# An encoder block on one core: output weights summed by transfers in DRAM instead of on VectorE, a fixed order for the opening, and a new table for the scan's order

## The chip, the cores and the metric

The kernel runs on one core of a Trainium2 chip. The metric is the device time of one execution in microseconds (us). Five engines with their own instruction queues matter here: TensorE (PE), VectorE (DVE), ScalarE (ACT), GpSimd (POOL) and SyncE (SP, which only issues transfers). Sixteen DMA engines serve the transfers that SP, ACT and POOL issue.

## The reference

One layer of a hybrid encoder over 1040 tokens (16 learned meta tokens and 1024 frames) of width 1024, in float32:

```
h = concat(meta, x)
u = rmsnorm(h) ; proj = u @ w_in                   # q, k, v, o and gates of 4 + 4 heads
h_ml = mlstm(conv+silu(q,k), v, gates)             # heads 0..3, chunked state scan
h_rt = retention(rotary(q), rotary(k), v)          # heads 4..7, chunked state scan
mixed = concat(sigmoid(o) * norm(h_ml), silu(g) * norm(h_rt))
h = h + mixed @ w_out
h = h + (silu(conv(rmsnorm(h) @ w_up)) * (rmsnorm(h) @ w_gate)) @ w_down
out = rmsnorm(h)[16:]
```

## The kernel before

Each float32 operand of a large product is split into a high part (`hi`, rounded by a cast) and a low part (`lo`, the difference), and each product is three matmuls, hi x hi, hi x lo and lo x hi. The large products use a seven-product (Strassen-like) scheme on 2 x 2 blocks, so that sums of blocks of the weights and of the activations are needed beside the blocks.

The program has four stages. **The opening** (0 to about 57 us) loads x in five regions of tokens (`RNG`, regions 0 to 4), forms the rms norm of each region, scales it, casts it to the high part and subtracts for the low part, while PE forms the value product of head 4 (`pv`) and its q and k product (`pq`, weights `("q4", 0)` and `("q4", 1)`). PE begins with products of a zero tile (`zeros`). **The projection and scan stage** (to about 650 us) runs, for the heads in the order 4, 0, 1, 2, 3, 5, 6, 7, the products q, v and o; between them it deals the scans of the heads done so far: for each chunk of 128 tokens the scores `s`, the weighted scores `pt`, their split `ph` and `pl` (on POOL, L1636 and L1655), the split of the values `vh` and `vl` (on POOL, L1667 and L1668), the products `u` and `n`, and the state `C`. Which scan step stands between which matmuls is decided when the program is written, by a planner (`slot`, `tick`) that keeps an estimated load per engine and follows the table `RULES`: seven numbers for each pair (kind of product, head), among them how long a step may lag and how many steps may be dealt in one slot. Once dealt, each engine runs its instructions in that order. **The output projection** `w_out` follows, then the **feed-forward stage** to the end.

The seven-product scheme for `w_out` needs sums of blocks of its weights. Before, eight units `w_unit(k)`, k = 0 to 7, are dealt into the projection stage: each loads two pieces of `w_out` to SBUF (2 x 512 KB), adds four times 128 x 512 elements on DVE (L651, L652, L654, L655) and stores four sums of 256 KB to DRAM (L658), where the output projection reads them later. The sums for `w_down` are made in another way, by `wsum`, from about 900 us: three copies from DRAM to DRAM and four transfers that add to their destination, all issued by POOL (L674 and L667).

The splits of a weight piece are in `parts`: casts on ACT (L484) and subtractions on DVE (L489). In the opening `norm_sums(2, True)` folds the squares of region 2 on DVE (L890, L893), PE sums them over partitions (L848), ACT and DVE form 1/rms, PE spreads it (L861) and DVE scales x (L920); the low parts of region 2 are L936.

Of the kernel before, what the change touches and what calls it, by code (L numbers as in the profile page):

```python
# [17 lines left out]
P = 128  # L18
# [70 lines left out]
def body(ctx, tc, h_in, vecs, cst, mask_in, rot, w_v0, w_vp, w_g, w_out, w_up, w_gate, w_down, out):  # L89
# [14 lines left out]
    def after(later, first):  # L104
        dep(later, first, False)
# [212 lines left out]
    jslot = {}  # L318
    age = {}
    jfreed = [[0, 1], [2, 3]]  # L320
    jcap = [2]

    def job(nm, *srcs):
        jobs.append((nm, srcs))
        return len(jobs) - 1
# [155 lines left out]

    def parts(key, pairs, src):
        for i, (hi, lo) in enumerate(pairs):
            m = AC.copy(hi, src[:, i * HB:(i + 1) * HB])  # L484
            if not dealt[0]:
                after(m, last["first" if key[0] == "q4" else "raw" if key[2] == 4 else "late"])
        yield
        for i, (hi, lo) in enumerate(pairs):
            m = V.tensor_tensor(lo, src[:, i * HB:(i + 1) * HB], hi.bitcast(F32), ALU.subtract)  # L489
            if not dealt[0]:  # L490
                after(m, last["added"])
        done.add(key)
# [149 lines left out]
    def w_unit(k):
        js = [job(f"w{k + 8 * i}", w_out[k + 8 * i]) for i in range(2)]

        def make():
            def g():
                ask(js, True)
                yield from landed(*js)
                r1, r2 = (jget(j) for j in js)
                (v11, v21), (v12, v22) = ((r[:, :HB], r[:, HB:]) for r in (r1, r2))  # L650
                V.tensor_tensor(v22, v22, v21, ALU.add)  # L651
                V.tensor_tensor(v21, v21, v11, ALU.add)  # L652
                yield
                V.tensor_tensor(v11, v11, v22, ALU.add)  # L654
                V.tensor_tensor(v12, v12, v11, ALU.add)  # L655
                yield from lag(1.5)
                for x, st_, o in ((v22, "65", HB), (v21, "73", HB), (v11, "65", 0), (v12, "73", 0)):
                    nc.sync.dma_start(sums["w", st_, k][:, o:o + HB], x)  # L658
                yield from lag(4)
                jfree(*js)  # L660
            spawn(g())
        unit(("w", k), 0, make)
# [18 lines left out]

# [68 lines left out]
    wk_ = list(range(8))  # L750

    def w_units(n):
        return [lambda: w_unit(wk_.pop(0))] * n

    def m_units(h):
        return [lambda: m_unit(h)]
    u_fm("o", 4, *v_units(0, 0), *w_units(1))
    prev = 4
    for p, (a, b) in enumerate(PAIRS):
        u_fm("q", a)  # L760
        u_vp(p)
        u_fm("o", a, *v_units(p, 1), *m_units(prev), *w_units(1))
        u_fm("q", b, *(r_units(0, 1) if p == 2 else w_units(1)))
        u_fm("o", b, *(v_units(p + 1, 0) if p < 2 else r_units(2, 3)), *m_units(a), *w_units(p < 2))
        prev = b
    u_fm("q", 7, *r_units(4, 5))
    u_fm("v", 7, *r_units(6, 7))
# [105 lines left out]
    def norm_sums(r, late=False):  # L873
# [34 lines left out]
        norm_scale(r)  # L908
        norm_lows(r)

    def norm_scale(r):
        half, j0, j1 = RNG[r]
        if len(norms[r]) < 3:
            norm_rows(r)
        xs, got, pr = norms.pop(r)
        parts_ = [[u[:, :, j0:j1] for u in UB[f"{half + 1}{i + 1}"]] for i in range(2)]
        scaled[r] = xs, parts_
        for i, x in enumerate(xs):
            for k in range(4):
                last["scale"] = V.scalar_tensor_tensor(x[:, k], x[:, k], vec[:, V_MIX + 4 * i + k:V_MIX + 4 * i + k + 1], pr, ALU.mult, ALU.mult)  # L920
# [1047 lines left out]
    need(("q4", 1), 0)
    row.clear()
    quiet = last["added"]  # L1970
    raw_done(1, pv1, col0[:, 1:2])
# [7 lines left out]
    raw_done(2, pv2, col1[:, 0:1])  # L1979
    for i in range(2):  # L1980
        after(AC.copy(w0hi[i], w0raw[i]), last["cast"])
    pair = q4_pair(0, 0, 272, [next(ring0), next(ring0)], 2, third)
    next(pair)
    norm_scale(2)
# [798 lines left out]
```

## Time and profile before

| quantity | value |
|---|---|
| median of 3 runs | 1500.06 us (1500.03 to 1500.83) |
| profiled execution, its own time | 1501.6 us |
| its span in the trace | 1499.8 us |
| PE busy in the span | 1477.2 us (98%) |
| DVE, ACT, POOL busy | 74%, 51%, 13% |

The profile is of one execution; its own time is 1.8 us above its span and 1.5 us above the median of the runs. Busy time of PE counts matmuls that are pipelined, so that a busy PE can still run below its pace, at the lower of its two clocks for example.

### The profile page before, as it was taken

Reading aid. Unit: us, or ns where it says so; the run is one execution under the profiler, and the core shown is the slowest. Engines: PE = TensorE matmul, PEld = TensorE weight load, DVE = VectorE, ACT = ScalarE, POOL = GpSimd, SP = SyncE. Lnnn points to the kernel's source line nnn. Section 1 sums busy time; section 2 is a strip of 40 time slices with the busy share of each in tenths; the row PEclk is TensorE's granted clock in tenths of the full one; section 3 lists DMA queues with packets and bytes.
Section 4 is the critical chain, followed back from the end, with each engine's and each line's share of the span. In section 5 each row is a group of like instructions: output and inputs, shape, how many; then the busy total and the mean of one; then the engine's idle time right before and its main releaser. Section 6 shows DMA issues by size and latency. Waiting matters only on the chain.

```text
span 1499.8 us, 26297 instructions
## 1 busy us (share of the span) xinstructions
PE 1477.2 (98%) x10034; PEld 1342.3 (89%) x10034; DVE 1113.5 (74%) x2142; ACT 759.4 (51%) x1471; POOL 190.3 (13%) x406
## 2 busy tenths in 40 slices
PE   9999999999999999999999999999999999999997
PEld 7989999999899989987888999888888889888887
DVE  6987878788778776857867887666666666777667
ACT  6566555565555455544454664444444445444443
POOL 0003220314031303040000002222210000000000
PEclk9999999999999999999999999999999999999999
DMA  6021364224523354697333258888762225933313
GB/s 236 28 86 66 121 200 153 79 78 168 185 85 114 126 199 147 206 399 259 106 107 130 96 173 215 217 214 203 186 157 77 75 81 186 354 99 106 99 43 113
DMA packets 97758, 223.85 MB, mean 149 GB/s; under 512 B 10600, under 2 KB 25648, under 8 KB 97456
## 3 DMA queue, kind: packets, MB, share of 16 engines
q1 hardware_dynamic: 82992, 191.68, 37.7%
q0 software_dynamic: 8448, 23.07, 7.7%
q10 hardware_dynamic: 6192, 7.41, 1.4%
q8 instruction: 79, 1.29, 0.4%
q14 instruction: 47, 0.39, 0.1%
HBM read 178.05 MB, written 67.15 MB: 163 GB/s over the span
## 4 chain that ended last, share of the span: by engine, by line
PE 88%; DVE 7%; DMA 3%; issue 1%; ACT 1%; SPq 0%; DVEq 0%; POOL 0%; ACTq 0%
PE pdx L954 3%; PE pdx L953 3%; PE pdx L952 3%; PE pup_x L953 3%; PE pup_x L952 3%; PE pup_x L954 3%; PE pga_x L952 2%; PE pga_x L953 2%; PE pga_x L954 2%; PE pdy L954 2%; PE pdy L953 2%; PE pwx L954 2%; PE pdy L952 2%; PE pwx L952 2%; PE pwx L953 2%; PE n L1701 2%
## 5 line engine op out<-in xcount | busy, mean ns | idle before, releaser
L794 ACT CAST hi_up<-raw_up 128x512 fp32r<-128x512 f32 (+1 forms) x52 | 36.5, 720 | 110.2 <-PE pga_z L953 61.1
L795 DVE TENSOR_TENSOR lo_up<-raw_up,hi_up 128x512 fp32r<-128x512 f32 (+1 forms) x52 | 41.3, 808 | 38.4 <-ACT hi_up L794 37.6
L953 PE MATMUL pup_x<-ul_g,hi_up 128*128 128x256 f32 (+1 forms) x240 | 67.4, 282 | 0.0
L952 PE MATMUL pup_x<-uh_g,hi_up 128*128 128x256 f32 (+1 forms) x240 | 67.2, 282 | 0.0
L795 DVE TENSOR_TENSOR lo_ga<-fraw_ga,hi_ga 128x512 fp32r<-128x512 f32 (+1 forms) x51 | 40.6, 799 | 35.5 <-ACT hi_ga L794 35.3
L954 PE MATMUL pup_x<-uh_g,lo_up 128*128 128x256 f32 (+1 forms) x240 | 66.4, 282 | 0.0
L795 DVE TENSOR_TENSOR lo_d<-rd,hi_d 128x1024 fp32r<-128x1024 f32 (+1 forms) x34 | 37.6, 1112 | 32.8 <-ACT hi_d L794 32.7
L954 PE MATMUL pdx<-uh_d,lo_d 128*128 128x512 f32 (+1 forms) x156 | 57.9, 375 | 0.0
L794 ACT CAST hi_ga<-fraw_ga 128x512 fp32r<-128x512 f32 (+1 forms) x51 | 35.4, 713 | 44.4 <-PE pup_z L953 23.9
L953 PE MATMUL pdx<-ul_d,hi_d 128*128 128x512 f32 (+1 forms) x156 | 57.8, 374 | 0.0
L794 ACT CAST hi_d<-rd 128x1024 fp32r<-128x1024 f32 (+1 forms) x34 | 32.3, 960 | 48.2 <-PE pdy L953 32.5
L954 PE MATMUL pdy<-uh_d,lo_d 128*128 128x512 f32 x132 | 51.9, 393 | 0.0
L953 PE MATMUL pdy<-ul_d,hi_d 128*128 128x512 f32 x132 | 51.7, 392 | 0.0
L2650 POOL TENSOR_TENSOR resid<-resid,Rc 128x256 f32<-128x256 f32 x2 | 1.4, 716 | 381.3 <-ACT Rc L865 381.3
L674 POOL DMA_DIRECT2D wsd<-w_down_d x33 | 19.9, 746 | 231.0 <-DVE s2up L2408 230.8
L952 PE MATMUL pdx<-uh_d,hi_d 128*128 128x512 f32 (+1 forms) x156 | 48.5, 372 | 0.0
L1636 POOL CAST ph<-pt 128x128 fp32r<-128x128 f32 x64 | 20.0, 312 | 221.0 <-DVE pt L1644 132.9
L952 PE MATMUL pdy<-uh_d,hi_d 128*128 128x512 f32 x132 | 47.9, 389 | 0.0
L952 PE MATMUL pga_x<-uh_g,hi_ga 128*128 128x512 f32 x120 | 47.5, 396 | 0.0
L953 PE MATMUL pga_x<-ul_g,hi_ga 128*128 128x512 f32 x120 | 47.5, 396 | 0.0
L954 PE MATMUL pga_x<-uh_g,lo_ga 128*128 128x512 f32 x120 | 47.1, 393 | 0.0
L1668 POOL TENSOR_TENSOR vl<-v,vh 128x258 fp32r<-128x258 f32 (+1 forms) x48 | 36.1, 752 | 80.2 <-PE n L1675 54.0
(1737 smaller groups left out, 6020.4 us busy)
## 6 DMA issues: line engine op xcount, KB each, us to landing
raw_up<-w_up_d SPq DMA_DIRECT2D x22, 512.0 KB
fraw_ga<-w_gate_d SPq DMA_DIRECT2D x22, 512.0 KB
acts<-cv SPq DMA_DIRECT2D x44, 256.0 KB
wsd<-w_down_d POOLq DMA_DIRECT2D x44, 256.0 KB, 6.7
rd<-wsd SPq DMA_DIRECT2D x22, 512.0 KB
raw_w<-w_out_d SPq DMA_DIRECT2D x20, 512.0 KB
wsw<-raw_w SPq DMA_DIRECT2D x32, 256.0 KB
raw_m<-w_out_d SPq DMA_DIRECT2D x14, 512.0 KB
```

The source lines that it names most:

```text
L674: dep(G.dma_start(x, y), last["pace"], True)
L794: AC.copy(hi[:, o:o + n], x)
L795: V.tensor_tensor(lo[:, o:o + n], x, hi[:, o:o + n].bitcast(F32), ALU.subtract)
L952: m.append(PE.matmul(pt, ah, xh_, start=first and k == 0, stop=False, skip_group_check=True))
L953: PE.matmul(pt, ah, xl_, start=False, stop=False, skip_group_check=True)
L954: m.append(PE.matmul(pt, al, xh_, start=False, stop=last and k == n - 1, skip_group_check=True))
L1636: G.tensor_copy(ph, pt)
L1668: G.tensor_tensor(low, v, vh.bitcast(F32), ALU.subtract)
L1701: PE.matmul(pn[:L, :nv], qd, state["C"][:, :nv], start=False, stop=True)
L2650: nc.gpsimd.tensor_tensor(RES[mb][:, a0:t1], RES[mb][:, a0:t1], R[1], ALU.mult)
```

## The change

1. The eight `w_unit(k)` are gone from the projection stage. A new `w_sums(range(8))` stands in the opening, behind the low parts of region 2: 24 copies from DRAM to DRAM, issued by SP, each of which waits until DVE has written those low parts (`last["lows", 2]`), and 32 adding transfers, issued by POOL, in three rounds over the eight k.
2. The opening is written in one fixed order up to the squares of region 3: 11 products of zero rather than 13, the norm's sums of region 0 behind one product of the values rather than three, the low part of region 0's first half ahead of region 1's scaling, the fold of region 2 ahead of the splits of the q weights, the gates' scalings (`raw_g`) behind. The two casts of the first q weights go from ACT to POOL. Region 2 of x is loaded ahead of the second q weights.
3. 18 of the rows of `RULES` have other numbers, so that the planner deals the scan anew.

```diff
-    ('q', 0): (3, 0.5, 2.0, 2.0, 3, 1, 3),
+    ('q', 0): (3, 0.3, 4.5, 4.0, 3, 0, 3),
...
-    jcap = [2]
+    jcap = [1]
...
-            m = AC.copy(hi, src[:, i * HB:(i + 1) * HB])
+            m = G.tensor_copy(hi, src[:, i * HB:(i + 1) * HB]) if key == ("q4", 0) else AC.copy(hi, src[:, i * HB:(i + 1) * HB])
...
+    def w_sums(ks):
+        for k in ks:
+            d65, d73 = (sums["w", x, k] for x in ("65", "73"))
+            for x, y in ((d65, w_out[k]), (d73[:, HB:], w_out[k][:, HB:]), (d73[:, :HB], w_out[k + 8][:, :HB])):
+                dep(nc.sync.dma_start(x, y), last["lows", 2], True)
+        for step in range(3):
+            for k in ks:
+                d65, d73 = (sums["w", x, k] for x in ("65", "73"))
+                if step == 0:
+                    add(d65[:, HB:], w_out[k + 8][:, HB:])
+                    add(d73[:, HB:], w_out[k][:, :HB])
+                else:
+                    add((d65, d73)[step - 1][:, :HB], (d65[:, HB:], d65[:, :HB])[step - 1])
...
-    u_fm("o", 4, *v_units(0, 0), *w_units(1))
+    u_fm("o", 4, *v_units(0, 0))
...
     xload(2)
+    jcap[0] = 2
+    jload()
...
-    zeros(13)
+    zeros(11)
     pv1, pv0, pv2 = pp("pv4_1", next(ring0)), pp("pv4_0", next(ring0)), pp("pv4_2", next(ring0))
-    raw_value(pv1, xg0, META, (0, 1, 2))
+    raw_value(pv1, xg0, META, (0,))
...
     norm_lows(2)
-    next(pair, None)
     fourth = norm_sums(3, True)
     last["third"] = last["added"]
+    w_sums(range(8))
```

DVE in the opening, from the reciprocal of region 1's norm on; `u11l` and `u12l` are low parts, `sqr` the squares that are folded, `lo_q` the low parts of the q weights, `gts` the gates. Before:

```order
L852 RECIPROCAL rcola_229<-rcola_229 128x1
L1920 TENSOR_TENSOR x_129<-sig,pra_301 128x4x128
L1920 TENSOR_TENSOR x_128<-sig,pra_301 128x4x128
L1929 TENSOR_TENSOR u11l<-x_129,u11h 128x4x144
L1929 TENSOR_TENSOR u12l<-x_128,u12h 128x4x144
L1915 TENSOR_SCALAR gts<-pv_1_255,rcola_228 128x2x4
L1929 TENSOR_TENSOR u11l<-x_129,u11h 128x4x128
L1929 TENSOR_TENSOR u12l<-x_128,u12h 128x4x128
L489 TENSOR_TENSOR lo_q_0_0_324<-raw_q_0_213,hi_q_0_0_323 128x512 x2
L890 TENSOR_TENSOR sqr_139<-sqr_139,sqr_140 128x4x256
L893 TENSOR_TENSOR sqr_139<-sqr_139 128x2x256
L489 TENSOR_TENSOR lo_q_1_0_336<-raw_q_1_215,hi_q_1_0_335 128x512 x2
```

The same place of DVE in the changed program (whose lines have other numbers):

```order
L845 RECIPROCAL rcola_229<-rcola_229 128x1
L1929 TENSOR_TENSOR u11l<-x_129,u11h 128x4x144
L1920 TENSOR_TENSOR x_129<-sig,pra_304 128x4x128
L1920 TENSOR_TENSOR x_128<-sig,pra_304 128x4x128
L1929 TENSOR_TENSOR u12l<-x_128,u12h 128x4x144
L1929 TENSOR_TENSOR u11l<-x_129,u11h 128x4x128
L1929 TENSOR_TENSOR u12l<-x_128,u12h 128x4x128
L884 TENSOR_TENSOR sqr_139<-sqr_139,sqr_140 128x4x256
L887 TENSOR_TENSOR sqr_139<-sqr_139 128x2x256
L494 TENSOR_TENSOR lo_q_0_0_301<-raw_q_0_213,hi_q_0_0_300 128x512 x2
L845 RECIPROCAL rcola_358<-rcola_358 128x2
L494 TENSOR_TENSOR lo_q_1_0_330<-raw_q_1_219,hi_q_1_0_329 128x512 x2
```

One low part moved ahead of region 1's scaling; the fold (L884, L887) moved ahead of the first `lo_q`, and the gates' scaling is no longer in front of it.

POOL between the opening and the scan of head 4, from the second split of head 4's values on; `v_10` and `v_00` are value tiles of head 0. Before:

```order
L1667 CAST vh_2_1399<-v4lo 128x256
L1608 MEMSET vz 16x2
L1117 MEMSET v_10_1852 128x4x2
L1117 MEMSET v_00_1622 128x4x2
L1636 CAST ph_1_1362<-pt_1_1350 128x128
L1655 TENSOR_TENSOR pl_1_1363<-pt_1_1350,ph_1_1362 128x128
```

In the changed program 32 adding transfers stand between the same cast and `v_10`; these are the first of them:

```order
L1663 CAST vh_2_1425<-v4lo 128x256
L650 DMA wsw_0_159<-w_out_d 128x512
L650 DMA wsw_0_167<-w_out_d 128x512
L650 DMA wsw_1_160<-w_out_d 128x512
L650 DMA wsw_1_168<-w_out_d 128x512
L650 DMA wsw_0_159<-wsw_0_159 128x512
L1604 MEMSET vz 16x2
L650 DMA wsw_2_161<-w_out_d 128x512
L650 DMA wsw_2_169<-w_out_d 128x512
L650 DMA wsw_3_162<-w_out_d 128x512
L650 DMA wsw_1_160<-wsw_1_160 128x512
```

`ph_1`, which the scan's first product with whole chunks needs, now stands behind all 32. On PE that product, `n_1`, stands 24 rows nearer to the start of the program than before (row 476, not 500), most of them matmuls of 264 columns or fewer.

DVE in the o product of head 3, around the first evacuation of `po3y`; `raw_w` are the sums of `w_unit`. Before:

```order
L651 TENSOR_TENSOR raw_w_5258<-raw_w_5258,raw_w_5256 128x512
L652 TENSOR_TENSOR raw_w_5256<-raw_w_5256 128x512
L1047 TENSOR_TENSOR sig<-sig,po3y_5279 128x258
L489 TENSOR_TENSOR lo_o_4_0_5238<-raw_o3b,hi_o_4_0_5237 128x512
L654 TENSOR_TENSOR raw_w_5256<-raw_w_5256,raw_w_5258 128x512
L655 TENSOR_TENSOR raw_w_5258<-raw_w_5258,raw_w_5256 128x512
L1047 TENSOR_TENSOR sig<-sig,po3y_5301 128x256
L1232 SCALAR_TENSOR_TENSOR kT_5273<-rawk,vec,kT_5273 128x527
L1232 SCALAR_TENSOR_TENSOR kT_5273<-rawk,vec,kT_5273 128x526
L1232 SCALAR_TENSOR_TENSOR kT_5273<-rawk,vec,kT_5273 128x525
L489 TENSOR_TENSOR lo_o_4_0_5238<-raw_o3b,hi_o_4_0_5237 128x512
```

And in the changed program:

```order
L1228 SCALAR_TENSOR_TENSOR kT_5215<-rawk,vec,kT_5215 128x527
L1228 SCALAR_TENSOR_TENSOR kT_5215<-rawk,vec,kT_5215 128x526
L1228 SCALAR_TENSOR_TENSOR kT_5215<-rawk,vec,kT_5215 128x525
L1043 TENSOR_TENSOR sig<-sig,po3y_5277 128x258
L494 TENSOR_TENSOR lo_o_2_0_5149<-raw_o3a,hi_o_2_0_5148 128x512
L494 TENSOR_TENSOR lo_o_4_0_5234<-raw_o3b,hi_o_4_0_5233 128x512
L1043 TENSOR_TENSOR sig<-sig,po3y_5293 128x256
L494 TENSOR_TENSOR lo_o_4_0_5234<-raw_o3b,hi_o_4_0_5233 128x512
```

The four additions are gone from between the pieces of `lo_o`, and the convolution (L1232, now L1228) stands ahead of `po3y`. At the same place of head 6's o product the piece `lo_o_2` moved ahead of the evacuation of `po6y`, and a pair of instructions (a low part and a difference of `raw_fr`, 128 x 512 each) from ahead of it to behind it.

## Rows read from the trace of the kernel before

**Rows 1.** The page, busy time: us, share of the span, instructions.

```profile
PE 1477.2 (98%) x10034; PEld 1342.3 (89%) x10034; DVE 1113.5 (74%) x2142; ACT 759.4 (51%) x1471; POOL 190.3 (13%) x406
```

**Rows 2.** Windows by stage: stretch, its length, busy us of each engine, granted clock, DMA share.

```profile
0.00:115.00 115.00, 109.30 (x817) 101.19 (x818) 95.77 (x194) 67.16 (x127) 5.33 (x24) 0.99 0.36 123
...
160.00:750.00 590.00, 582.07 (x4436) 540.44 (x4435) 456.71 (x989) 314.11 (x640) 116.61 (x274) 1.00 0.49 165
750.00:1400.00 650.00, 649.96 (x3883) 576.36 (x3882) 468.54 (x776) 305.27 (x561) 54.14 (x77) 1.00 0.53 156
```

**Rows 3.** Timeline of PE, opening: start, us, instructions, idle time before and its releaser.

```profile
1.32 5.60 PE L1881 MATMUL pz<-zero 128*128 128x512 f32 x13 [1.32 <-POOL gts L290]
22.26 1.05 PE L848 MATMUL pca<-cs,sqr 128*128 128x1 f32 x8 [0.89 <-DVE sqr L893]
35.91 1.47 PE L848 MATMUL pca<-cs,sqr 128*128 128x1 f32 x12 [0.44 <-DVE sqr L893]
```

**Rows 4.** Windows behind two idle times of PE; the clock is the third number from the end.

```profile
23.00:27.00 4.00, 4.00 (x21) 4.00 (x22) 1.75 (x6) 2.26 (x3) 0.67 (x1) 0.57 0.79 289
560.00:570.00 10.00, 9.28 (x59) 8.36 (x58) 5.92 (x16) 2.73 (x8) 2.44 (x6) 0.83 0.31 105
```

**Rows 5.** Timeline of DVE, opening.

```profile
14.63 1.28 DVE L1920 TENSOR_TENSOR x<-sig,pra 128x512 f32<-128x512 f32 x2 [0.70 <-PE pra L861]
15.84 1.30 DVE L1929 TENSOR_TENSOR u11l<-x,u11h 128x576 fp32r<-128x576 f32 x1
17.06 0.75 DVE L1929 TENSOR_TENSOR u12l<-x,u12h 128x576 fp32r<-128x576 f32 x1
17.73 0.21 DVE L1915 TENSOR_SCALAR gts<-pv,rcola 128x8 f32<-128x8 f32 x1
...
19.07 1.28 DVE L489 TENSOR_TENSOR lo_q<-raw_q,hi_q 128x512 fp32r<-128x512 f32 x2
...
21.52 0.69 DVE L893 TENSOR_TENSOR sqr<-sqr 128x512 f32<-128x512 f32 x1
...
32.58 1.22 DVE L936 TENSOR_TENSOR u12l<-x,u12h 128x1024 fp32r<-128x1024 f32 x1
```

**Rows 6.** Timeline of ACT, then of POOL, opening.

```profile
16.48 1.14 ACT L484 CAST hi_q<-raw_q 128x512 fp32r<-128x512 f32 x2
...
15.79 0.73 POOL L1668 TENSOR_TENSOR vl<-v4lo,vh 128x256 fp32r<-128x256 f32 x1
```

**Rows 7.** Timeline of PE, o products of heads 3 and 6.

```profile
399.82 0.39 PE L954 MATMUL po3y<-uS1h,lo_o 128*128 128x258 f32 x1 [1.80 <-DVE lo_o L489]
...
556.46 0.39 PE L954 MATMUL po6x<-uS2h,lo_o 128*128 128x258 f32 x1 [2.07 <-DVE lo_o L489]
562.00 0.39 PE L954 MATMUL po6y<-uS1h,lo_o 128*128 128x258 f32 x1 [0.72 <-DVE lo_o L489]
```

**Rows 8.** The tile raw_w: durations in ns, min, median, max; first and last start.

```profile
L651 DVE TENSOR_TENSOR raw_w<-raw_w,raw_w x8: 679/687/727, 168.4 to 528.1; 128x512 f32<-128x512 f32 x8
```

**Rows 9.** The page, DMA queue of POOL: packets, MB, share of 16 engines' span.

```profile
q0 software_dynamic: 8448, 23.07, 7.7%
```

**Rows 10.** Timeline of POOL: an adding transfer and the next, which waits for it.

```profile
1106.24 0.81 POOL L667 DMA_DIRECT2D wsd<-wsd  x1 [4.80 <-DMA wsd<-w_down_d]
1111.38 0.83 POOL L667 DMA_DIRECT2D wsd<-wsd  x1 [4.34 <-DMA wsd<-wsd]
```

**Rows 11.** Windows from the low parts of region 2 to the scan of head 4.

```profile
31.00:70.00 39.00, 38.40 (x319) 37.84 (x317) 37.39 (x65) 16.46 (x28) 0.09 (x1) 1.00 0.01 2
70.00:107.00 37.00, 34.59 (x290) 32.91 (x291) 33.20 (x79) 25.94 (x51) 0.10 (x1) 1.00 0.31 101
```

**Rows 12.** Timeline of POOL, then of PE: chunk 1 of head 4.

```profile
110.49 0.29 POOL L1636 CAST ph<-pt 128x128 fp32r<-128x128 f32 x1
...
113.05 0.28 PE L1674 MATMUL n<-vh,ph 128*128 128x256 f32 x1
113.17 0.28 PE L1675 MATMUL n<-vl,ph 128*128 128x256 f32 x1
```

More of the change, by code (lines that the diff above doesn't have):

```diff
@@ L384, in body @@
     evacs = []
+    held = []
     dealt = [False]
@@ L396, in spawn @@
                 owner[id(g)] = key
+        elif held:
+            next(g)
+            held[0].append(g)
         else:
@@ L483, in parts @@
         for i, (hi, lo) in enumerate(pairs):
-            m = AC.copy(hi, src[:, i * HB:(i + 1) * HB])
+            m = G.tensor_copy(hi, src[:, i * HB:(i + 1) * HB]) if key == ("q4", 0) else AC.copy(hi, src[:, i * HB:(i + 1) * HB])
             if not dealt[0]:
-                after(m, last["first" if key[0] == "q4" else "raw" if key[2] == 4 else "late"])
+                if not (held or key == ("q4", 0)):
+                    after(m, last["first" if key[0] == "q4" else "raw" if key[2] == 4 else "late"])
         yield
@@ L640, in m_unit @@
         unit(("m", h), 0, make)
[L642 to L662, printed above, removed]
     sums = {(g, st_, k): dram.tile([P, 2 * HB], F32, name=f"ws{g}{st_}_{k}") for g, n in (("w", 8), ("d", KD)) for st_ in ("65", "73") for k in range(n)}
@@ L749, in body @@
     u_load(("q4", 1), q4[:, 3 * HB:], q4[:, :HB])
-    wk_ = list(range(8))
-    def w_units(n):
-        return [lambda: w_unit(wk_.pop(0))] * n
     def m_units(h):
         return [lambda: m_unit(h)]
-    u_fm("o", 4, *v_units(0, 0), *w_units(1))
+    u_fm("o", 4, *v_units(0, 0))
     prev = 4
@@ L761, in body @@
         u_vp(p)
-        u_fm("o", a, *v_units(p, 1), *m_units(prev), *w_units(1))
-        u_fm("q", b, *(r_units(0, 1) if p == 2 else w_units(1)))
-        u_fm("o", b, *(v_units(p + 1, 0) if p < 2 else r_units(2, 3)), *m_units(a), *w_units(p < 2))
+        u_fm("o", a, *v_units(p, 1), *m_units(prev))
+        u_fm("q", b, *(r_units(0, 1) if p == 2 else ()))
+        u_fm("o", b, *(v_units(p + 1, 0) if p < 2 else r_units(2, 3)), *m_units(a))
         prev = b
@@ L885, in norm_sums @@
         else:
-            after(AC.activation(sq[1], xs[1], AF.Square), last["sqrt"])
+            last["squares"] = AC.activation(sq[1], xs[1], AF.Square)
+            after(last["squares"], last["sqrt"])
         if r == 1:
@@ L909, in norm_split, with norm_scale @@
         norm_lows(r)
-    def norm_scale(r):
+    def norm_scale(r, hook=None):
         half, j0, j1 = RNG[r]
@@ L919, in norm_scale @@
             for k in range(4):
+                if i and k == 0 and hook:
+                    hook()
                 last["scale"] = V.scalar_tensor_tensor(x[:, k], x[:, k], vec[:, V_MIX + 4 * i + k:V_MIX + 4 * i + k + 1], pr, ALU.mult, ALU.mult)
@@ L1887, in region @@
         half, j0, j1 = RNG[r]
-        return [xf[f"{half + 1}{i + 1}"][:, :, j0:j1] for i in (0, 1)], [x[:, :, j0:j1] for x in sqs], tmp.tile([P, 5], F32, tag="rcol", name=f"rcola{r}")
+        return [xf[f"{half + 1}{i + 1}"][:, :, j0:j1] for i in (0, 1)], [x[:, :, j0:j1] for x in sqs], (tmp if r else st).tile([P, 5], F32, tag="rcol" if r else "rraw", name=f"rcola{r}", bufs=2 if r else 1)
     row.append({})
@@ L1911, in raw_meta, with raw_v, raw_g @@
             PE.matmul(pv0[32 * j:32 * j + 32, :264], xg0[i][:, j, :32], w0raw[i][:, j * 264:(j + 1) * 264], start=i == 0, stop=i == 1, tile_position=(0, 32 * j))
-    def raw_done(c, pv, col):
+    def raw_v(c, pv, col):
         AC.activation(vtile[4][0][:, (c - 1) * VW:(c - 1) * VW + DV], pv[:, :DV], AF.Copy, scale=col)
+    def raw_g(c, pv, col):
         V.tensor_scalar(gts[:, :, c, :], pv[:, DV:264].rearrange("p (a b) -> p a b", a=2), col, None, ALU.mult)
@@ L1940, in body @@
     AC.activation(q1[1], x1[1], AF.Square)
-    raw_value(pv1, xg0, META, (3,))
-    raw_meta(0, (0, 1))
+    raw_value(pv1, xg0, META, (1,))
     pr0 = rms_rows(got0, None, "upd")
-    raw_meta(0, (2, 3))
+    raw_value(pv1, xg0, META, (2, 3))
+    raw_meta(0, range(4))
     weighted(xg1, x1, range(4))
@@ L1954, in body @@
     weighted(xg1, x1, (6, 7))
+    low_half(0, 0)
     cast_half(0, 1)
+    held[:] = [[]]
+    issue(1)
+    rest = held.pop()
     pr1 = rms_rows(got1, None, "num")
@@ L1960, in body @@
         cast_half(1, i)
-    for r in range(2):
-        for i in range(2):
-            low_half(r, i)
+    for r, i in ((0, 1), (1, 0), (1, 1)):
+        low_half(r, i)
     raw_value(pv2, xg1, 0, range(8))
     last["first"] = last["cast"]
-    need(("q4", 0), 0)
     third = norm_sums(2, True)
[L1968 to L1971, printed above, removed]
+    held[:] = [[]]
+    issue(2)
+    rest += held.pop()
     t0_ = vz[:META, 264:2 * 264]
@@ L1978, in meta_done, with whole, q4_pass @@
         V.tensor_copy(gts[:META, :, 0, :], t0_[:, DV:].rearrange("p (a b) -> p a b", a=2))
-    raw_done(2, pv2, col1[:, 0:1])
-    for i in range(2):
[L1981 to L1984, printed above, removed]
+    def whole(g):
+        for _ in g:
+            pass
+    qt = [next(ring0), next(ring0)]
+    w = [ready["q4", i] for i in range(2)]
+    pq = [pp(f"pq4{i}00", qt[i])[:, :272] for i in range(2)]
+    def q4_pass(p, i, ks):
+        a, b = ((0, 0), (0, 1), (1, 0))[p]
+        for kb in ks:
+            u = UB[f"1{kb // 4 + 1}"][b]
+            PE.matmul(pq[i], w[i][kb // 4][a][:, kb % 4 * P:(kb % 4 + 1) * P], u[:, kb % 4, :272], start=p + kb == 0, stop=p == 2 and kb == KB - 1, skip_group_check=True)
+    raw_v(1, pv1, col0[:, 1:2])
+    AC.copy(w0hi[0], w0raw[0])
+    raw_v(2, pv2, col1[:, 0:1])
+    for i in range(2):
+        q4_pass(0, i, range(8))
+    q4_pass(1, 0, range(0))
+    whole(rest[0])
+    third()
+    whole(rest[1])
+    AC.copy(w0hi[1], w0raw[1])
+    q4_pass(1, 0, range(0, 8))
+    q4_pass(1, 1, range(0))
+    norm_rows(2)
+    norm_scale(2, lambda: (raw_g(1, pv1, col0[:, 1:2]), raw_g(2, pv2, col1[:, 0:1])))
+    q4_pass(1, 1, range(0, 8))
+    for i in range(2):
+        q4_pass(2, i, range(8))
+    row.clear()
+    AC.copy(raws[0][:, :272], pq[0])
+    after(AC.copy(raws[1][:, :272], pq[1]), last["cast"])
     for i in range(2):
@@ L1993, in body @@
         after(V.tensor_copy(ug[:, 4 * i:4 * i + 4], x[:, :, :META]), last["third"])
-    for c in (3, 4):
-        v4_group(c, next(ring0))
-    pair = q4_pair(0, 272, SB, [next(ring0), next(ring0)], 3, fourth)
+    v4_group(3, next(ring0))
+    v4_group(4, next(ring0), fourth)
+    pair = q4_pair(0, 272, SB, [next(ring0), next(ring0)], 3, lambda: None)
     next(pair)
```

30 rows, old and new, of the table RULES are left out of this document.

## The prediction

> **What bounds the kernel now.** I read the page first, then windows by stage, then the timeline of each engine where PE is idle. On the page PE is busy for 1477.2 of 1499.8 us [rows 1]; what any change can give back is thus some 22 us of idle time, and the stretches in which PE is busy at its lower clock. The windows say where the idle time lies: 115 - 109.3 = 5.7 us before 115 us, 590 - 582.07 = 7.9 us from 160 to 750 us, and nothing in the feed-forward stage, 649.96 of 650 us [rows 2]. So only the opening and the projection stage can pay.
>
> In the opening PE spends 5.60 us on 13 zero products (0.43 us each), and waits twice for a fold of squares on DVE, 0.89 us before 22.26 and 0.44 us before 35.91 [rows 3]. Behind the first wait the granted clock falls: from 23 to 27 us it is 0.57 on average, so part of that time is at the lower level, 1.2 rather than 2.4 GHz, and 4 x (1 - 0.57) = 1.7 us of full-clock work are lost [rows 4]. In the projection stage the largest waits are for low parts of o weights from DVE: 1.80 us at 399.82, 2.07 at 556.46, 0.72 at 562.00 [rows 7]; behind the last two a window of 10 us has the clock at 0.83, again 1.7 us lost [rows 4].
>
> **The opening.** What PE waits for at 22.26 is L893, which ends at 21.52 + 0.69 = 22.21 [rows 5]. In the new order of DVE the idle 0.70 us before 14.63 is filled by a low part that stood behind it, the gates' 0.21 us and the two q splits of 1.28 us come after the fold instead of before it [rows 5]: 2.19 us. The squares that the fold reads must come earlier too; ACT loses the 1.14 us of casts to POOL [rows 6] and one evacuation of values to a later place. Two zero products fewer start everything at most 0.86 us earlier, of which I take 0.3 us, since the norm's sums wait for x and its squares as well. The fold is then done 2.5 us earlier. The gates and q splits that were moved must be done before or between the scalings of region 2, where DVE before waited for PE, so I let the whole 2.5 us reach the second fold at 35.91. From there to 70 us DVE is busy for 37.4 of 39 us [rows 11], and a shift of its chain shifts PE. Bounds: only the wait of 0.89 us goes (PE was slowed by its clock there and not only by the order), or both waits, the lost clock and the two zero products all go: 0.89 + 0.44 + 1.7 + 0.86 = 3.9 us. I take 2.5: it is what the chain gives, and lies between.
>
> One thing speaks against it. POOL's subtraction at 15.79 lasts until 16.52 [rows 6], and the DVE subtraction that starts at 15.84 lasts 1.30 us, where the same shape lasts 0.75 at 17.06 [rows 5]: the two delayed one another by 0.55 us. Moved to POOL, the two q casts can do the same to the folds of regions 0 and 1, once or twice, 0.55 to 1.1 us; one such loss is there already, so I leave it inside the bounds. By the Trainium skill (SBUF — State Buffer, Who interferes with whom) a VectorE instruction with two SBUF inputs contends with a GpSimd instruction that reads SBUF, and one of them blocks for the whole of the other; the trace agrees with the 1.30 against 0.75 us. By that rule alone the opening would give 1.4 us rather than 2.5.
>
> **The w units.** 32 additions of about 0.69 us [rows 8] leave DVE, 22 us, and 16 loads and 32 stores leave SP. Most of this was hidden: DVE is busy for 457 of 590 us there [rows 2] and PE waits only where DVE's order puts a needed low part behind other work. At 399.82 the four additions (2.75 us) stand in front of that low part; without them the wait of 1.80 us goes. At 556.46 no `w_unit` is near, but in the new order a pair of 128 x 512 instructions (2 x 0.69 = 1.4 us) and an evacuation come behind `lo_o_2`; 2.07 us shrink to about 0.3, and with it goes the loss of clock, 1.7 us. Together 1.8 + 1.8 + 1.7 = 5.3 us. A new deal makes waits of its own, which no trace shows: nothing at least, and at most as many as now, 7.9 us [rows 2]. I charge 1.5 us, since most of the 7.9 us are in the places named. Net 3.8 us; from 6.3 us (all three waits, 4.6, and the clock, 1.7, and nothing new) to a loss of 2 us.
>
> **The sums in DRAM.** Copies start when the low parts of region 2 are written, 32.58 + 1.22 = 33.8 [rows 5], less 2.5: at 31.3 us. The DMA engines are idle then (share 0.01 from 31 to 70 us [rows 11]), so the copies alone cost nothing. Their price is in who waits behind them. POOL must issue 32 adding transfers in order, most of which wait for an earlier one, before it comes to `ph_1`. The same work for `w_down`, 11 groups of three copies and four additions, is POOL's whole queue before: 7.7% of the span, 115 us of all 16 engines, 10.5 us a group [rows 9]. Eight groups are 84 us, so they end at 115. One addition takes 1111.38 - 1106.24 = 5.1 us from issue to the release of the next [rows 10]; POOL would have issued the last about 4.3 us before the end, at 111. It is needed when? `n_1` stands at 113.05 now [rows 12]; the opening brings it to 110.55, and the 24 rows fewer ahead of it (0.12 us each by the two rows) by another 2.8 to 107.7; `ph_1` takes 0.29, so POOL must be free by 107.4. That is 3.6 us too late, all of it idle time of PE, which runs in order. [...] From above the loads of 70 to 107 us, 0.31 x 37 = 11.5 us of all engines [rows 11], are in the way as well: POOL free at 122.5, 15.1 us late. I take 2 us, near the lower half, since half of the stretch has no other traffic.
>
> **Sum.** -2.5 - 3.8 + 2 = -4.3 us. Against the profiled execution 1501.6 - 4.3 = 1497.3; the median of the runs stands 1.5 us lower, so 1500.06 - 4.3 = 1495.8 us.
>
> **Rivals.** (a) *POOL's queue decides.* The additions run at the rate of the whole queue and share with the loads, POOL comes to `ph_1` at 122.5, and PE idles 15.1 us at `n_1`: 1500.06 - 2.5 - 3.8 + 15.1 = 1508.9. The point from which the kernel is slower than before is POOL free at 107.4 + 6.3 = 113.7 us. For it: 10.5 us a group is a measured price; the loads for head 0 must pass through the same engines. Against it: an idle stretch of 39 us at the start. By the Trainium skill (DMA: Bandwidth & Descriptors, Queues, rings and completion order) each DMA engine takes turns between the queues that have work, packet by packet, so that these loads would be slowed by the additions too; no row here shows the shares.
>
> (b) *The gains don't arrive.* The fold is earlier, but PE waits as long one step further on (for the scaled region 2, which needs the q splits done first), 0.9 us gained; the new deal has waits of the size of the old, 0.5 gained; POOL costs 1: 1500.06 - 0.4 = 1499.7, no change. For it: DVE is full from 31 to 70 us, so work moved within it is not removed. Against it: 22 us of DVE work are really removed.
>
> (c) *More than forecast*: opening 3.9, middle 6.3, POOL nothing: 1489.9.
>
> **How the numbers follow.** The forecast and its neighbours (1492 to 1498) get 0.52, (c) and near it 0.12, (b) 0.13, (a) and what lies between it and no change 0.23. The range for 8 in 10 goes from (c)'s 1489.9, say 1489.5, to 1504, half of (a)'s loss: beyond are some 0.12 above and 0.05 below. The likeliest case's own range is 1492 to 1498. What a measurement of this kernel can tell from no change is about 0.2%, 3.0 us: below 1497.06 is faster, which takes most of the forecast's chance and all of (c), 0.60; same 0.16; slower 0.24.
>
> **What would show it.** Right: the fold of region 2 ends near 19.7 us and no stretch at the lower clock follows; PE's second fold sums stand near 33.4; no wait of 1.8 us at the o product of head 3 and none over 0.5 at head 6's; POOL issues its last adding transfer before about 109 us and `ph_1` follows when the scores are there. Wrong: a wait of PE for POOL at `n_1` of several us, a DVE wait for A or raw_q0b between 70 and 90 us, because loads come late beside the additions; or new waits for low parts from the new table that add up to more than 4 us.

## The result, and the profile after

The changed kernel takes 1504.12 us (median of 8 runs, 1501.83 to 1507.68), the kernel before 1500.05 us (8 runs on the same chip). The ratio is 1.0028, 95% interval 1.0016 to 1.004: slower by about 0.3%, where I had forecast 1495.8 us and faster. The profiled execution took 1503.68 us with a span of 1501.9 us.

The page of the changed kernel: first busy us, share and instructions of each engine (to be held against [rows 1]), then the granted clock and the DMA share in 40 slices of 37.5 us, then the two large DMA queues (packets, MB, share; [rows 9] has q0 before).

```profile
PE 1475.5 (98%) x10032; PEld 1342.3 (89%) x10032; DVE 1092.0 (73%) x2110; ACT 755.8 (50%) x1468; POOL 216.9 (14%) x440
...
PEclk9999999999999999999999999999999999999998
DMA  7993233223312235697333258888762225933213
...
q1 hardware_dynamic: 78640, 183.29, 36.1%
q0 software_dynamic: 13056, 31.46, 11.2%
```

PE has less to do than before, 1475.5 for 1477.2 us, in a longer span: the loss is idle time and clock. The second and third slices of DMA (37 to 113 us) are full; they are the place to look. The windows by stage of the changed kernel, columns as in [rows 2]:

```profile
0.00:115.00 115.00, 104.85 (x776) 96.29 (x776) 92.88 (x185) 64.50 (x121) 30.72 (x49) 0.97 0.94 247
160.00:750.00 590.00, 588.84 (x4532) 549.62 (x4531) 441.46 (x970) 321.75 (x659) 114.85 (x275) 1.00 0.41 139
750.00:1400.00 650.00, 649.96 (x3884) 576.36 (x3883) 468.51 (x777) 305.25 (x561) 54.12 (x77) 1.00 0.54 156
...
75.00:115.00 40.00, 33.77 (x254) 31.35 (x253) 29.08 (x76) 20.25 (x42) 15.64 (x19) 0.96 0.99 201
115.00:160.00 45.00, 38.48 (x294) 37.39 (x295) 26.73 (x64) 22.28 (x44) 15.76 (x37) 0.92 0.30 79
...
5.00:10.00 5.00, 3.96 (x19) 2.87 (x18) 2.83 (x5) 3.37 (x11) 0.00 (x0) 0.85 1.08 367
10.00:15.00 5.00, 5.00 (x26) 3.55 (x27) 2.94 (x6) 2.86 (x10) 1.38 (x2) 0.81 1.05 370
...
85.00:90.00 5.00, 3.43 (x17) 3.43 (x18) 4.74 (x14) 2.94 (x7) 1.49 (x3) 0.70 1.03 221
...
120.00:125.00 5.00, 3.76 (x16) 3.55 (x17) 1.34 (x5) 0.37 (x1) 3.30 (x9) 0.55 1.08 293
```

From 160 to 750 us PE is idle for 1.16 us, before for 7.93 [rows 2]: that part of the change works better than forecast. Before 160 us it is the reverse: 6.2 us idle from 75 to 115, 6.5 from 115 to 160, and behind both holes the clock is down (0.70 and 0.55). The DMA share before 115 us went from 0.36 to 0.94.

The timeline of PE in the changed kernel names the holes (columns as in [rows 3]):

```profile
1.32 4.53 PE L1879 MATMUL pz<-zero 128*128 128x512 f32 x11 [1.32 <-POOL zero L289]
...
34.71 1.47 PE L841 MATMUL pca<-cs,sqr 128*128 128x1 f32 x12 [0.45 <-DVE sqr L887]
...
86.57 0.39 PE L948 MATMUL po4x<-uS3h,hi_o 128*128 128x256 f32 x1 [4.64 <-ACT sig L1041]
...
121.24 0.58 PE L1670 MATMUL n<-vh,ph 128*128 128x256 f32 x1 [6.81 <-POOL ph L1632]
```

**The second hole** is what I had named rival (a): POOL comes to `ph_1` late. Its timeline, to be held against [rows 10, 12]:

```profile
114.01 0.83 POOL L650 DMA_DIRECT2D wsw<-wsw  x1 [0.30 <-issue]
119.97 0.82 POOL L650 DMA_DIRECT2D wsw<-wsw  x1 [5.13 <-issue]
120.50 0.46 POOL L1113 MEMSET v<- 128x8 f32 x2
120.89 0.29 POOL L1632 CAST ph<-pt 128x128 fp32r<-128x128 f32 x1
```

The 32 additions are issued from 37.16 to 119.97 us; POOL is free at 120.5, where the upper bound in my prediction said 122.5.

**The first hole** begins with a load. Timelines of SP (issue of the copies, then of the two halves of A_4), DVE and ACT in the changed kernel:

```profile
32.63 30.92 SPq L667 DMA_DIRECT2D wsw<-w_out_d  x24
68.71 0.34 SPq L1175 DMA_DIRECT2D A<-rot_d  x1
69.88 0.33 SPq L1176 DMA_DIRECT2D A<-rot_d  x1
...
80.35 0.71 DVE L1252 TENSOR_TENSOR qT<-rawq,A 128x528 f32<-128x528 f32 x1 [3.39 <-DMA A<-rot_d]
83.03 0.71 DVE L1253 TENSOR_TENSOR kT<-kT,A 128x528 f32<-128x528 f32 x1 [1.97 <-DMA A<-rot_d]
...
81.15 0.63 ACT L1249 COPY rawq<-rawk 64x528 f32<-64x528 f32 x1 [3.83 <-DVE qT L1252]
...
85.94 0.31 ACT L1287 ACTIVATE gates<-gates 36x128 f32<-36x128 f32 x1 [1.84 <-DVE gates L1286]
86.16 0.36 ACT L1041 ACTIVATE sig<-po4x 128x256 f32<-128x256 f32 x1
```

A_4 is two transfers of 520 KB. The first is issued at 68.71 and lets DVE go on at 80.35 only, while copies and additions have the DMA engines full; DVE waits for it and for the second half, ACT's copy and its activation of the gates wait for DVE, and the activation that would empty `po4x` stands behind both on ACT, so PE waits.

### The profile page after: what moved, and what is told of

It is laid out like the page before. It is cut to its first block, busy times and chain, and to the rows that moved or that the text cites. A ratio compares the mean times of both kernels' runs of the same rounds, so it can differ in the third digit from the quotient of the medians.

```text
span 1501.9 us, 26232 instructions
## 1 busy us (share of the span) xinstructions
PE 1475.5 (98%) x10032; PEld 1342.3 (89%) x10032; DVE 1092.0 (73%) x2110; ACT 755.8 (50%) x1468; POOL 216.9 (14%) x440
## 4 chain that ended last, share of the span: by engine, by line
PE 90%; DVE 6%; DMA 2%; ACT 1%; issue 1%; SPq 0%; DVEq 0%; POOL 0%; POOLq 0%; ACTq 0%
PE pdx L950 3%; PE pdx L949 3%; PE pdx L948 3%; PE pup_x L949 3%; PE pup_x L948 3%; PE pup_x L950 3%; PE pga_x L948 2%; PE pga_x L949 2%; PE pga_x L950 2%; PE pdy L950 2%; PE pdy L949 2%; PE pwx L950 2%; PE pdy L948 2%; PE pwx L948 2%; PE pwx L949 2%; PE n L1697 2%
## 5 line engine op out<-in xcount | busy, mean ns | idle before, releaser
L788 DVE TENSOR_TENSOR lo_up<-raw_up,hi_up 128x512 fp32r<-128x512 f32 (+1 forms) x52 | 41.4, 810 | 38.3 <-ACT hi_up L787 37.5
L949 PEld LDWEIGHTS pup_x<-ul_g,hi_up 128*128 128x128 f32 x240 | 45.4, 189 | 0.9 <-DVE ul_g L2206 0.2
```

The source lines that it names most:

```text
L788: V.tensor_tensor(lo[:, o:o + n], x, hi[:, o:o + n].bitcast(F32), ALU.subtract)
L949: PE.matmul(pt, ah, xl_, start=False, stop=False, skip_group_check=True)
```

## The experiments

Two theories stood at the start. **A**: the sums in DRAM are the loss, by the time that their transfers take of the DMA engines (A_4 late) and by POOL, which is held in its queue until 120.5 us; opening and scan order gain. **B**: the waits come from the new order itself and the sums lie beside it. All medians and ratios are against runs of the kernel before on the same chip (medians 1499.9 to 1500.3).

**1. No sums.** The sums are left out and the output projection reads unsummed rows:

```diff
-    w_sums(range(8))
...
-                nc.sync.dma_start(x[:, :2 * HB], sums[self.nm, st, k])
+                nc.sync.dma_start(x[:, :2 * HB], w_out[k + 8 * (st == "73")] if self.nm == "w" else sums[self.nm, st, k])
```

> The changed kernel without its 24 copies and 32 additions; the products of the output weights read unsummed rows of w_out in their place (that part of the computation is left out), with as many loads of the same size. Opening and scan order are the changed ones. Theory A (the sums in DRAM hold POOL until 120.5 us and keep the DMA engines full, so that A_4 comes late): both waits of TensorE go, 6.81 us at n_1 and 4.64 us at po4x, and with them the low clock behind them (about 3 us): 1488 to 1491 us. Rival B (the waits come from the new order of the opening, the sums only lie beside them): at least one of the waits stays: 1495 to 1504 us.

Measured: 1490.71 us, ratio 0.9935 (0.9923 to 0.9947). Both holes are gone; windows of 75 to 160 us:

```profile
75.00:115.00 40.00, 36.88 (x287) 34.14 (x287) 31.79 (x84) 22.59 (x48) 3.36 (x9) 1.00 0.31 104
115.00:160.00 45.00, 44.72 (x367) 43.90 (x366) 33.47 (x74) 31.43 (x62) 12.34 (x29) 1.00 0.15 49
```

Against the changed kernel PE has 3.1 us more in the first window and 6.2 in the second, at full clock. B is out: the sums cost 1504.12 - 1490.71 = 13.4 us.

**2. Copies alone.** The sums are not computed; the output projection reads what the copies left:

```diff
+    COPIES_ONLY = True
...
+                if COPIES_ONLY:
+                    continue
```

> The changed kernel with the 24 copies but none of the 32 additions (the sums are left out of the computation). Theory A, in the form that the additions alone hold POOL and carry the DMA load past 64 us: no wait for POOL at n_1, A_4 lands within 3 us of its issue, 1488 to 1491 us. Rival C (the copies' backlog delays A_4 and the loads of q0): the 6.8 us at n_1 go, the 4.6 us at po4x stay: about 1494 to 1496 us.

Measured: 1488.62 us, ratio 0.9919 (0.9906 to 0.9932). The copies cost nothing: the DMA share is 0.15 from 60 to 64 us and 0.00 from 64 to 68, so they are through when A_4 is issued at 69.42. Rival C is out. The DMA queue's row of this kernel from 34 to 62 us, and below it the two queues of the changed kernel from 70 to 115 us (packets, MB, share of 16 engines):

```profile
q1 hardware_dynamic: 2554, 8.26, 91.6%
```

```profile
q0 software_dynamic: 2784, 5.06, 70.4%
q1 hardware_dynamic: 1544, 4.27, 28.6%
```

This gives prices. A copy of 256 KB (0.262 MB) takes 0.916 x 28 / 8.26 x 0.262 = 0.81 us of all 16 engines; an addition of the same size 0.704 x 45 / 5.06 x 0.262 = 1.64 us, twice as much. The eight groups are 8.39 MB of copies, 26 us, and 8.39 MB of additions, 52 us.

**3. The opening alone**, with the units, the old table and no sums in DRAM:

```diff
-    ('o', 0): (4, 0.8, 3.0, 3.0, 4, 0, 1),
+    ('o', 0): (4, 0.3, 3.0, 2.5, 2, 0, 3),
...
+    u_fm("o", 4, *v_units(0, 0), *w_units(1))
...
-    w_sums(range(8))
```

> The changed opening alone: the units that make the sums on VectorE, and the scan order of before, are put back, and no sums in DRAM. Theory A: 1497 to 1499 us, since TensorE's rows up to 69 us stood 2.1 us ahead of before's in the changed kernel. My prediction's term for this part was 2.5 us (1497.5). Rival: the opening brings nothing by itself, as the clock of 0.81 to 0.85 between 5 and 15 us takes it back: 1500 us.

Measured: 1498.29 us (12 runs), ratio 0.9984 (0.9975 to 0.9992): 1.8 us by the medians, 2.4 (1.2 to 3.7) by the ratio. The 12 runs lie between 1495.72 and 1501.63 us, and the profiled one is the slowest of them; its clock is low from 5 to 15 us:

```profile
5.00:10.00 5.00, 3.76 (x18) 2.64 (x16) 2.84 (x5) 2.83 (x10) 0.00 (x0) 0.82 1.08 375
10.00:15.00 5.00, 5.00 (x20) 3.07 (x19) 2.74 (x4) 2.28 (x7) 1.91 (x2) 0.50 1.04 368
```

**4. The same work in two late bursts.**

```diff
-    w_sums(range(8))
...
+            plan.append((COPY_AT + 10.0 * i, lambda k=k: copies(k)))
+            plan.append((ADD_AT[0] + 3.5 * i, lambda k=k: adds(k, 0)))
...
+    COPY_AT = 130 - OFF
+    ADD_AT = [x - OFF for x in (220, 382, 398)]
```

> The changed kernel with the same 24 copies and 32 additions, put later: copies by SP from about 130 to 200 us, additions by POOL from about 220 and from about 382 us, where it has no work of a scan. Theory A: the cost was the place, not the work; as without the sums plus 1 us: 1488 to 1492 us, so faster than both kernels. Rival D (the transfers cost wherever they are, since 16.8 MB more delays the weight loads of 130 to 420 us): new waits for DMA there, 1495 us or more.

Measured: 1500.56 us (12 runs), ratio 0.9999 (0.9989 to 1.0009). Theory A in this form fell: 16 additions in a row make loads late at 220 us as they do in the opening. The rows of ACT and PE there, with DMA queue q0 from 225 to 250 us:

```profile
245.37 0.62 ACT L488 CAST hi_q<-raw_q2a 128x512 fp32r<-128x512 f32 x1 [5.47 <-DMA raw_q2a<-w_g_d]
247.37 0.49 PE L1629 MATMUL s<-qT,kT 128*128 128x128 f32 x2 [3.54 <-DVE pt L1659]
```

```profile
q0 software_dynamic: 1422, 2.59, 72.3%
```

The additions took 72% of the DMA engines (1.83 us each), the weights of the next q were late, and PE waited 3.5 us for `pt`, which stood on DVE behind the low part of these weights. Behind the second burst PE waits 2.3 us more, at 419 us. So the place mattered less than the burst; D, a cost of each single transfer, was next.

**5 and 6. One by one.** Copies in the opening, as changed; the additions from the list below, at modelled times of PE, each tied to PE's last instruction at that time. Run 5 lists 32 times in stretches in which POOL has no scan, 4 us or more apart; run 6 one every 15 us, scans or not:

```diff
-    w_sums(range(8))
+    w_copies(range(8))
...
+    w_adds([x - 61 for x in range(140, 612, 15)])
```

> Copies in the opening as in the changed kernel; the 32 additions one by one, 6 us or more apart, from 152 to 610 us, in the stretches in which POOL has no work of a scan. Theory A, mended after the late burst (an addition takes DMA time for itself, and only a burst of them makes loads late and holds POOL): no wait of TensorE over 1 us between 75 and 640 us, 1488 to 1492 us, faster than both kernels. Rival D (each addition still delays a load that something waits for): some ten new waits of half a microsecond, 1493 to 1498 us.

> As the spread one, but one addition every 15 us from 140 to 605 us, scans included. Theory A: 1488 to 1492 us, since POOL's queue is never full and one issue takes it under 1 us. Rival E (POOL must not be interrupted within a scan, however short): a wait of about 1 us for each of some 16 additions that fall into scans: 1496 to 1506 us.

Measured: 1492.52 us, ratio 0.9953 (0.9941 to 0.9966), and 1491.36 us, ratio 0.9941 (0.9927 to 0.9954). Run 6 computes everything and is faster than both kernels, by 8.5 and 12.8 us. Run 5 lies 0.5 us above theory A's range. D and E are out: no wait of PE behind 75 us is over 1 us in either. What run 6 takes more than the runs without additions is 0.7 us (run 1) or 2.7 us (run 2); the intervals of the three overlap. In run 6 the additions take, from 140 to 610 us:

```profile
q0 software_dynamic: 4608, 8.39, 12.8%
...
wsw<-w_out_d POOLq DMA_DIRECT2D x16, 256.0 KB, 4.5
```

that is 0.128 x 470 / 32 = 1.88 us each. They cost the DMA engines as much as in the burst; they are only never in front of a load for long.

**7. Half of the groups** in the opening; the other four sums are left out and read unsummed.

```diff
-                nc.sync.dma_start(x[:, :2 * HB], sums[self.nm, st, k])
+                nc.sync.dma_start(x[:, :2 * HB], w_out[k + 8 * (st == "73")] if self.nm == "w" and k > 3 else sums[self.nm, st, k])
...
-    w_sums(range(8))
+    w_sums(range(4))
```

> The changed kernel with four of the eight groups summed in its opening (12 copies, 16 additions); the other four are left out of the computation and read unsummed. Theory A (POOL's queue): at about 2.6 us an addition the last is issued near 80 us, so POOL is free long before n_1 and the 6.8 us go; A_4 meets the last four additions only and waits 0 to 2 us: 1489 to 1492 us. Rival F (the cost follows the work, half of 13.4 us): 1497 us.

Measured: 1490.85 us, ratio 0.994 (0.9926 to 0.9954), the same as without sums. F, a cost in proportion to the work, is out: there is a point up to which the sums are free.

**8. Units with the new table.** Run 3 with the changed rows of `RULES` (they are 16, not 18 as said above):

```diff
-    ('o', 0): (4, 0.3, 3.0, 2.5, 2, 0, 3),
+    ('o', 0): (4, 0.8, 3.0, 3.0, 4, 0, 1),
...
```

> The changed opening and the changed scan order, but with the units that make the sums on VectorE put back and no sums in DRAM. Theory G (the 7.6 us between the opening alone and the kernel without sums come from the missing units): 1496 to 1500 us. Rival H (they come from the new table of the scan order, which also removes the waits with the units in): 1490 to 1493 us.

Measured: 1516.95 us, ratio 1.0112 (1.0097 to 1.0126), worse than either theory. The largest wait of PE is 8.3 us for DVE's `vz`. With the units in, the new table is a loss of 18.7 us against run 3, so by itself it is no gain. The old table without the units was not run, so how much of run 1's gain over run 3 is work removed, and how much a better order, stays open.

**9. Two steps of three in the opening**, the last 8 additions one by one from 160 us.

```diff
-        for step in range(3):
+        for step in range(2):
...
+    w_adds([x - 61 for x in range(160, 600, 60)])
```

> The changed kernel with the copies and the first two steps of the sums (24 additions) in its opening, and the last step's 8 additions one by one from 160 to 580 us. POOL is then free some 10 to 15 us earlier (its last addition of the second step was issued near 105 us), while the transfers beside A_4 stay as they were. Theory A (two causes, DMA beside A_4 and POOL's queue): the 4.6 us at po4x stay, the 6.8 us at n_1 go or shrink below 2: 1495 to 1498 us. Rival I (POOL's queue is the only cause that counts; the late A_4 is taken back before 120 us): 1490 to 1493 us.

Measured: 1495.15 us, ratio 0.9957 (0.9943 to 0.997), with the first hole alone. PE's timeline has two waits over 1 us from 60 to 160 us, and POOL is early at `ph_1`:

```profile
86.49 0.58 PE L966 MATMUL po4x<-uS3h,hi_o 128*128 128x256 f32 x1 [6.16 <-ACT sig L1059]
...
118.01 0.49 PE L1628 MATMUL s<-qT,kT 128*128 128x128 f32 x2 [1.41 <-DVE kl L1654]
```

```profile
101.90 0.82 POOL L650 DMA_DIRECT2D wsw<-wsw  x1 [0.44 <-issue]
...
112.57 0.11 POOL L1131 MEMSET v<- 128x8 f32 x1 [7.17 <-DMA scr<-gates]
112.61 0.29 POOL L1650 CAST ph<-pt 128x128 fp32r<-128x128 f32 x1
```

I is out: with POOL early the first hole stays. With 24 additions in the opening the kernel stands 4.4 us above run 1 (1495.15 - 1490.71); the last 8 bring another 9.0 (1504.12 - 1495.15). By the ratios it is 3.3 and 10.6. The 4.4 go with late A_4. The 9.0 are not shown to be POOL's queue alone, since run 9 takes the transfers of the last 8 out of this stretch as well. Another load is late there, `raw_vp`. ACT's cast of it, ahead of the scan's next `kw` on ACT, in the changed kernel and in run 9:

```profile
117.70 1.14 ACT L488 CAST hi_vp<-raw_vp 128x512 fp32r<-128x512 f32 x2 [5.13 <-DMA raw_vp<-w_vp_d]
```

```profile
115.90 1.14 ACT L488 CAST hi_vp<-raw_vp 128x512 fp32r<-128x512 f32 x2 [3.42 <-DMA raw_vp<-w_vp_d]
```

In run 9 DVE waits for that `kw`, and PE for DVE, the 1.41 us at 118.01. In the changed kernel the cast comes 1.8 us later, hidden behind the wait for POOL. An estimate from these two rows: some 1.8 of the 9.0 us would have stayed had only POOL been free. No run separates the two.

**10. The first casts of q's weights on ScalarE again**, on top of run 6:

```diff
-            m = G.tensor_copy(hi, src[:, i * HB:(i + 1) * HB]) if key == ("q4", 0) else AC.copy(hi, src[:, i * HB:(i + 1) * HB])
+            m = AC.copy(hi, src[:, i * HB:(i + 1) * HB])
```

> The evenly spread kernel with the first two casts of q's weights back on ScalarE. My prediction gave the casts on POOL a part of the 2.5 us of the opening, less what VectorE loses beside POOL (lo_q 2.02 us for 1.28). If moving them was worth something: 1492 to 1494 us; if VectorE's loss eats it: 1490 to 1492 us, the same as the evenly spread one.

Measured: 1492.9 us, ratio 0.995 (0.9937 to 0.9962), against 0.9941 (0.9927 to 0.9954): the intervals overlap, so this can't be told from nothing. `lo_q` on DVE takes 2.02 us here too, so it is not the casts on POOL that make it 2.02.

**11. All copies and half of the additions in the opening**, the other half one every 30 us:

```diff
+    w_copies(range(8))
+    w_first(range(4))
...
+    w_adds([x - 61 for x in range(140, 612, 30)])
```

> All copies and four groups' 16 additions in the opening, the other 16 additions one by one every 30 us from 140 to 590 us. By theory A neither part costs more than 1 us: 1488.5 to 1491.5 us, the fastest whole kernel; if each spread addition costs what it seems to (1491.4 with 32, 1488.6 with none, so 0.09 us each), 1490.

Measured: 1496.29 us (10 runs), ratio 0.9974 (0.9965 to 0.9984): a miss. PE waits 3.30 us at `po4x` again, and DVE for A_4:

```profile
84.40 0.58 PE L971 MATMUL po4x<-uS3h,hi_o 128*128 128x256 f32 x1 [3.30 <-ACT sig L1064]
```

```profile
77.90 0.71 DVE L1275 TENSOR_TENSOR qT<-rawq,A 128x528 f32<-128x528 f32 x1 [4.19 <-DMA A<-rot_d]
```

The prices fit the row of cases. The transfers start near 32 us and the engines are full while they last, so by the prices they end near 58 us with the copies alone (32 + 26, run 2), 71 with half of both (32 + 13 + 26, run 7), 84 in run 11 (32 + 26 + 26), 97 in run 9 (32 + 26 + 39) and 110 in the changed kernel (32 + 78), each later by the loads that pass, up to 11.5 us [rows 11]. In windows of 4 us the DMA share falls below one half behind 60, 84, 92, 104 and 124 us in these five.

A_4 is issued between 67 and 70 us in all of them. DVE's first instruction that needs it starts 5.8 us after the issue in run 2, where it doesn't wait for it, and 7.4, 10.1, 13.2 and 11.6 us after it in runs 7, 11, 9 and the changed kernel: late wherever transfers are still under way then, and the later the more of them there are. Run 9 and the changed kernel had the same ones beside A_4 and differ by 1.5 us. PE's own wait (none, 0.56, 3.30, 6.16 and 4.64) also depends on when PE comes to `po4x`, at 80.33 us in run 9 and at 81.93 in the changed kernel.

## Why the prediction was wrong

**The step that failed is the size of "the sums in DRAM".** I took 2 us; it was 13.4. The numbers that I had worked out were near: POOL free at 111, at most 122.5 (it was 120.5), `n_1` at 107.7 without a wait (109.70 in run 1). What failed is the choice between the ends, "I take 2 us, near the lower half, since half of the stretch has no other traffic". No run shows 2 us for 32 additions in a row behind the copies. The stretch from 31 to 70 us was no reserve for the additions: the 24 copies of the same change fill 26 us of it. I had written that "the copies alone cost nothing", which run 2 shows to be true, and then left them out of the time of the additions behind them. An issue of 0.83 us is also no measure of such a transfer. By the Trainium skill (Perfetto Trace Analysis, DMA Instruction — SWDGE (GPSIMD)) the shown end of such an instruction on GpSimd is the writing of its last descriptor and not the end of the data; the trace agrees: the row is 0.8 us long, the data land 4.5 us after the issue in run 6, and take 1.88 us of all engines.

**A term was missing.** I named a wait for A between 70 and 90 us only as a sign of being wrong and gave it no price; it cost about 4.4 us (run 9 against run 1). By the Trainium skill (DMA: Bandwidth & Descriptors, Queues, rings and completion order), whose rule the prediction cites under rival (a), loads would be slowed and not held until the additions end. The trace agrees with it: A_4 came 11.6 us after its issue, 40 us before the additions were all issued.

**The opening** was right in size, in part by luck: 2.5 us forecast, 1.8 (2.4, 1.2 to 3.7, by the ratio) measured in run 3. Its first sign was met where the clock held. The end of the fold of region 2 in the timeline of DVE, in run 6 and in the changed kernel (before: [rows 5]):

```profile
18.94 0.69 DVE L900 TENSOR_TENSOR sqr<-sqr 128x512 f32<-128x512 f32 x1
```

```profile
20.56 0.69 DVE L887 TENSOR_TENSOR sqr<-sqr 128x512 f32<-128x512 f32 x1
```

In run 6 it ends at 19.63 us, with 19.7 forecast, and the second fold sums stand at 33.09, for 33.4. In the changed kernel's profiled execution the fold ends at 21.25 and the second sums stand at 34.71, where the clock was at 0.85 and 0.81 from 5 to 15 us, behind short waits for loads at 6.45 and 7.57. In run 3's it ends at 22.91, later than before (22.21), with the clock at 0.82 and 0.50. There the clock's loss had moved rather than gone, which the forecast left out; how often that happens to one program, the profiles, one of each, can't tell. The contention that I feared from the casts on POOL is not shown (run 10).

**The w units and the new order** were right in sign and half in size: 3.8 us forecast, 7.6 measured (run 1 against run 3). Of the 7.93 us of idle time only 1.16 stayed, where I had kept 1.5 for new waits and given back two waits and one loss of clock: the wait at head 3 is gone, that at head 6 is 0.32 us (I had said 0.3), and the small ones went too. The low end that I gave this term, a loss of 2 us, is 2.6 by its own numbers (5.3 - 7.9). With the terms as measured the sum is -1.8 - 7.6 + 13.4 = +4.0 us. That it meets the measured time proves nothing, since each term is the difference between neighbouring runs; it shows which term was off.

**Rival (a)** came nearest. POOL was free at 120.5, well behind its point of decision, 113.7. Its time, 1508.9, was too high, in part because it was set against the forecast's gain of the middle, 3.8 for 7.6. With the two gains as measured, 1.8 and 7.6, it would have given 1505.8. For its wait of 15.1 us at `n_1` the trace has 6.81: `n_1` stood 2.0 us later than forecast even without the sums (run 1), and the first hole, which (a) had not foreseen, had held PE up by 4.64 before. The range ended at 1504.0, just below 1504.12; half of (a)'s loss, by which it was set, is 4.4 us and would have put its end at 1504.5.

## What to carry to other kernels

Price a transfer by what it takes of the DMA engines, from the queue's share and its megabytes, and not by its issue: then add up all that is queued ahead of the next load that somebody needs. A stretch with idle DMA engines is a budget in microseconds of full engines; it is spent once, first by whatever is issued first, and beyond it the loads that pass are late, and so, here, was the engine that issued the additions in order. The same 32 additions and 24 copies cost 13.4 us with the additions in a burst, and 0.7 us with one addition every 15 us (run 6 against run 1; 2.7 against run 2).

## What the runs showed of the hardware

- A transfer that adds to its destination, DRAM to DRAM, takes 1.64 to 1.88 us of all 16 DMA engines per 256 KB in the stretches above (runs 4, 6 and the changed kernel), a copy 0.81 us (run 2). The queue's row of before [rows 9] holds a mean of the two, 0.077 x 1499.8 / 23.07 x 0.262 = 1.31 us, which hid it.
- While the engines are full, POOL's next addition follows about 2.5 us after the last (82.24, 84.80, 87.46, 90.00, 92.28 us in the changed kernel), although the instruction is shown for 0.81 us and the profile mostly names nothing that it waits for ("issue"). What holds POOL in between was not settled.
- The clock in the opening is not the same in all profiled executions, though the changed opening is written alike in them (but for the casts of run 10): from 5 to 10 and from 10 to 15 us it is 0.85 and 0.81 in the changed kernel, 0.82 and 0.50 in run 3, 1.00 and 0.66 in run 7, but 1.00 in both in run 6 (and in runs 4, 5 and 8 to 11). The rows of run 6 are below. Between the changed kernel and run 6 the fold moves by 1.6 us, most of what the change of the opening is worth. Each program was profiled once, so what decides it stays open.

```profile
5.00:10.00 5.00, 4.36 (x23) 2.97 (x22) 3.15 (x6) 3.50 (x12) 0.00 (x0) 1.00 1.07 378
10.00:15.00 5.00, 5.00 (x36) 3.36 (x35) 4.14 (x8) 3.61 (x10) 1.27 (x2) 1.00 1.05 376
```
